# Attention scores contracted over 128 partitions: q's two parts stacked, k's parts doubled, the missing half moved by DMA

## The chip, the cores and the metric

The kernel runs on one core of one Trainium2 chip. The metric is the device time of one execution in microseconds (us); three runs of the kernel before gave 2463.12, 2464.26 and 2464.34 us, so its time is 2464.26 us (median). A profiled execution of it took 2464.76 us.

## The reference

Two transformer blocks run over 512 tokens of width 1024, in float32. The first block mixes with two attentions, a windowed one with grouped heads and a neighbourhood one on a grid of 8 by 64 tokens, and ends in a feed-forward layer. The second has two layers of feed-forward, mixing and feed-forward; each mixing has a causal windowed attention beside a short convolution. Every head has 64 channels (`HEAD_DIM = 64`), every attention has 8 query heads, and the windowed ones have 2 key heads.

```python
def windowed_gqa(q, k, v, sink):            # first block
    ...
        sc = jnp.einsum('bqkgd,bskd->bkgqs', qi, ki).astype(jnp.float32) * scale
...
def neighborhood_attn(q, k, v, rpb):        # first block, 8 key heads
    ...
        sc = jnp.einsum('bchd,brckhd->bhcrk', qr, kn).astype(jnp.float32) * scale
...
def sliding_window_attention(q, k, v, sink):   # second block, each of two layers
    ...
    scores = jnp.einsum("bnqkgd,bnskd->bnkgqs", qb, k_band).astype(jnp.float32) * scale
```

## The kernel before, in words

Activations lie transposed: channels on the 128 partitions, 512 tokens along the free dimension. Every float32 operand of a matmul is split into a high part (rounded to the `fp32r` type by a ScalarE copy) and a low part (what is left, a VectorE subtraction), and a product is the sum of three matmuls: high by high, high by low, low by high. Weights are streamed from HBM in one fixed order (`MIX1_HEAD`, `FILL_AB`, `MIX2_HEAD`, `FILL_C` and others, lines 66 to 78), split the same way (ACT line 376, DVE line 378) some 5 half tiles ahead, and used once.

A linear layer's output tile (`Tile`, lines 450 to 452) is 128 channels by 512 tokens: 8 chunks of the inner dimension, 3 matmuls of 128 rows and 512 columns each. Such a tile of q holds two heads, one on partitions 0 to 63 and one on 64 to 127. `ev_split` (line 859) evacuates it: VectorE multiplies by the norm's factor (`scaled`, lines 846 and 848, or `scaled_by_columns`, line 854), ScalarE rounds the high part (line 553) and VectorE subtracts the low part (line 554). Both parts go into slots, tiles of 128 by 512 named r0 to r51.

Attention is done in steps, each of two heads (index g) and one block of 128 queries: 16 steps each for the windowed attention of the first block ("a"), for the neighbourhood one ("b"), and for each layer of the second block ("c0", "c1"). `qk` (line 704) makes the scores:

```python
for g in range(2):
    r = slice(HD * g, HD * g + HD)
    qs = slice(P * i, P * i + P)
    for j, (a, b) in enumerate(((qh, kh), (qh, kl), (ql, kh))):
        nc.tensor.matmul(sp[:, g, :w], a[r, qs], b[r, sl], start=(j == 0), stop=(j == 2))
```

So a step has six matmuls of 64 rows, three on the upper and three on the lower half of the partitions, with w = 256 columns in a head's first and last block of "a" and "b" and in all of "c", and 384 in the other two blocks of "a" and "b". Then VectorE adds the bias and takes the row's maximum (line 722), ScalarE takes the exponential (line 741), VectorE normalizes (line 749), TensorE transposes (line 758), the two parts are split (lines 553 and 554), and TensorE multiplies by v (line 778).

`run_attention` (line 787) writes the order out. Between the parts of the steps it puts pieces of the linear layers that are due (the "fillers", a quarter of a tile at a time, `halves`), in the order of `FILL_AB` or `FILL_C`, shared evenly over the steps by their cost. Before the first step it puts `2 * head` such quarters. The transposes of a step come one step after its scores in "a" and "b" (`LAG1 = 1`), two steps after in "c" (`LAG2 = 2`). A finished filler is evacuated at the next call of `evacuate`, at the latest just before a step that needs it. Each engine runs its own instructions in the order in which this code issues them.

The head of a mixing stage is `linear2` (line 515): q's first tile, k's tile and v's are made together, with the norm's factor (`inv`) ready only in the middle of v's. GpSimd's queue (POOL) issues the loads of "b"'s bias table (`rpb_load`, line 990), one per block, and later the reloads of x (line 1037).

## Time and profile before

| what | value |
|---|---|
| time, median of 3 runs (lowest to highest) | 2464.26 us (2463.12 to 2464.34) |
| the profiled execution's own time | 2464.76 us |
| its span in the trace | 2463.0 us |
| TensorE busy | 2436.1 us, 99% of the span |
| VectorE busy | 1960.7 us, 80% |
| ScalarE busy | 1261.0 us, 51% |
| GpSimd busy | 24.6 us, 1% |
| granted TensorE clock, mean over the span | 0.996 |

The span is that of the trace; what lies around it makes the execution's own time. Busy shares are of the whole span. Matmuls are pipelined, so one's duration is longer than the step from its start to the next one's, and a busy TensorE is not one at its peak. DVE is VectorE, ACT is ScalarE, PE is TensorE with PEld its weight loads.

### The profile page before, as it was taken

What the parts mean: (1) busy time and instruction counts of PE and PEld (TensorE: products, weight loads), DVE (VectorE), ACT (ScalarE), POOL (GpSimd) and SP (SyncE); (2) the same over time, 40 slices, a digit from 0 to 9 for tenths busy, and PEclk for the clock granted to TensorE, in tenths of its full rate; (3) what the DMA queues carried; (4) which work ended last, traced back from release to release, by engine and by line L of the source; (5) the groups of instructions that cost most, each with busy time, mean ns of one, the idle gap of its engine ahead of it and who ended that gap; (6) DMA issues with size and microseconds to landing.
All of it is one profiled execution on the core that took longest, in us unless ns stands there. A gap on an engine that the chain in (4) does not pass through costs nothing.

```text
span 2463.0 us, 39488 instructions
## 1 busy us (share of the span) xinstructions
PE 2436.1 (99%) x15098; PEld 2167.0 (88%) x15098; DVE 1960.7 (80%) x3943; ACT 1261.0 (51%) x2744; POOL 24.6 (1%) x37
## 2 busy tenths in 40 slices
PE   8999999999999999999999999999999999999998
PEld 6888888999879999988899999899999878999997
DVE  7778678877679878768798888898887687988885
ACT  5554355544455545544565445665445455654454
POOL 2000000000000000000000000000000000000000
PEclk9999999999999999999999999999999999999999
DMA  4222432233322332332223323323333322233332
GB/s 161 69 92 88 118 114 82 94 101 100 106 85 91 101 115 88 114 95 69 84 80 103 107 99 101 102 93 112 98 104 106 102 69 77 75 107 108 106 94 79
DMA packets 73901, 239.45 MB, mean 97 GB/s; under 512 B 8320, under 2 KB 10384, under 8 KB 73712
## 3 DMA queue, kind: packets, MB, share of 16 engines
q1 hardware_dynamic: 70496, 228.10, 29.0%
q0 software_dynamic: 1776, 7.27, 1.0%
q8 instruction: 118, 1.93, 0.3%
q10 hardware_dynamic: 1440, 1.57, 0.2%
q14 instruction: 71, 0.58, 0.1%
HBM read 234.81 MB, written 2.10 MB: 96 GB/s over the span
## 4 chain that ended last, share of the span: by engine, by line
PE 93%; DVE 5%; ACT 1%; issue 0%; DMA 0%; SPq 0%; DVEq 0%; ACTq 0%
PE X L1084 7%; PE X L1083 7%; PE X L1082 7%; PE YZ L1082 5%; PE YZ L1083 5%; PE YZ L1084 5%; PE mlp_D L451 2%; PE mlp_D L450 2%; PE mlp_D L452 2%; PE 0, 'ffn2'_D L450 2%; PE 1, 'ffn1'_D L450 2%; PE 0, 'ffn1'_D L450 2%; PE 0, 'ffn1'_D L451 2%; PE 0, 'ffn2'_D L451 2%; PE 1, 'ffn1'_D L451 2%; PE 0, 'ffn1'_D L452 2%
## 5 line engine op out<-in xcount | busy, mean ns | idle before, releaser
L378 DVE TENSOR_TENSOR wl<-raw,wh 128x512 fp32r<-128x512 f32 (+2 forms) x890 | 531.7, 609 | 98.3 <-ACT wh L376 91.4
L376 ACT CAST wh<-raw 128x512 fp32r<-128x512 f32 (+2 forms) x890 | 469.6, 555 | 8.4 <-DMA raw<-in_w 2.6
L1082 PE MATMUL X<-r,wh 128*128 128x256 f32 x1568 | 445.2, 284 | 3.8 <-ACT g L1088 3.6
L1084 PE MATMUL X<-r,wl 128*128 128x256 f32 x1568 | 444.0, 283 | 0.0
L1083 PE MATMUL X<-r,wh 128*128 128x256 f32 x1568 | 443.9, 283 | 0.0
L376 ACT CAST wh<-s 128x512 fp32r<-128x512 f32 x392 | 242.7, 620 | 224.6 <-DVE s L355 219.2
L1082 PE MATMUL YZ<-r,wh 128*128 128x256 f32 x1176 | 334.4, 284 | 0.8 <-ACT u L1094 0.8
L1083 PE MATMUL YZ<-r,wh 128*128 128x256 f32 x1176 | 333.3, 283 | 0.0
L1084 PE MATMUL YZ<-r,wl 128*128 128x256 f32 x1176 | 333.2, 283 | 0.0
L378 DVE TENSOR_TENSOR wl<-s,wh 128x512 fp32r<-128x512 f32 x392 | 268.8, 686 | 69.5 <-ACT wh L376 67.6
L1082 PEld LDWEIGHTS X<-r,wh 128*128 128x128 f32 x1568 | 300.1, 191 | 15.2 <-ACT g L1088 4.0
L1083 PEld LDWEIGHTS X<-r,wh 128*128 128x128 f32 x1568 | 300.1, 191 | 10.3 <-issue 1.2
L1084 PEld LDWEIGHTS X<-r,wl 128*128 128x128 f32 x1568 | 300.2, 191 | 0.0
L1082 PEld LDWEIGHTS YZ<-r,wh 128*128 128x128 f32 x1176 | 226.3, 192 | 1.6 <-ACT u L1094 1.4
L1083 PEld LDWEIGHTS YZ<-r,wh 128*128 128x128 f32 x1176 | 226.3, 192 | 0.2 <-issue 0.2
L1084 PEld LDWEIGHTS YZ<-r,wl 128*128 128x128 f32 x1176 | 226.3, 192 | 0.0
L1096 ACT COPY g<-X 128x256 f32<-128x256 f32 x98 | 36.5, 372 | 141.6 <-PE X L1084 141.5
L1097 DVE TENSOR_TENSOR u<-u,g 128x256 f32<-128x256 f32 x98 | 41.6, 424 | 75.8 <-ACT g L1096 75.8
L450 PE MATMUL mlp_D<-r,wh 128*128 128x512 f32 x256 | 100.1, 391 | 0.0
L451 PE MATMUL mlp_D<-r,wh 128*128 128x512 f32 x256 | 100.1, 391 | 0.0
L452 PE MATMUL mlp_D<-r,wl 128*128 128x512 f32 x256 | 99.6, 389 | 0.0
L1092 ACT COPY u<-X 128x256 f32<-128x256 f32 x98 | 36.5, 373 | 101.0 <-PE X L1084 101.0
(429 smaller groups left out, 5258.9 us busy)
## 6 DMA issues: line engine op xcount, KB each, us to landing
raw<-in_w SPq DMA_DIRECT2D x320, 512.0 KB, 3.7
raw<-in_w SPq DMA_DIRECT2D x64, 384.0 KB, 3.5
raw<-in_w SPq DMA_DIRECT2D x32, 448.0 KB, 3.5
raw<-in_w SPq DMA_DIRECT2D x32, 320.0 KB, 2.9
raw<-in_w SPq DMA_DIRECT2D x28, 256.0 KB, 2.6
bb<-in_rpb POOLq DMA_DIRECT2D x12, 384.0 KB, 3.3
xt<-in_x POOLq DMA_DIRECT2D x8, 256.0 KB, 2.9
xt<-in_x SPq DMA_DIRECT2D x1, 1024.0 KB, 12.7
```

The source lines that it names most:

```text
L376: nc.scalar.copy(h[:, :w], src)
L378: nc.vector.tensor_tensor(lo[:, :w], src, h[:, :w].bitcast(F32), ALU.subtract)
L450: nc.tensor.matmul(self.ps, h[:, c], hx, start=(self.n == 1), stop=False)
L451: nc.tensor.matmul(self.ps, h[:, c], lx, start=False, stop=False)
L452: nc.tensor.matmul(self.ps, lo[:, c], hx, start=False, stop=end)
L1082: nc.tensor.matmul(out, h[:, c], hx, start=first, stop=False, skip_group_check=skip)
L1083: nc.tensor.matmul(out, h[:, c], lx, start=False, stop=False, skip_group_check=skip)
L1084: nc.tensor.matmul(out, l[:, c], hx, start=False, stop=(k == 3), skip_group_check=skip)
L1092: nc.scalar.copy(u[:, lo], out)
L1096: nc.scalar.copy(g[:, hi], out)
L1097: nc.vector.tensor_tensor(u[:, hi], u[:, hi], g[:, hi], ALU.add)
```

## The change

The product of q and k is written differently. For a head g, one slot now holds q's high part on the head's own 64 partitions and q's low part on the other 64; two slots hold k's high part on both halves and k's low part on both halves. A score is then two matmuls over 128 rows (stacked q by high k, stacked q by low k), which sum all four products of parts instead of three. The halves that the evacuation writes stay where the channels are; the other halves are copied across partitions by DMAs that GpSimd issues (`move`): two per tile of q, four per tile of k, each of 64 partitions by 512 elements (128 KB). A tile of q or k is now rounded and subtracted in two operations of 64 partitions instead of one of 128, and k takes four slots instead of two.

With it come a new order (k ahead of q at the head of a stage and in `FILL_AB`, with the tiles of "b" made earlier) and `head=3` instead of 1: six quarters of fillers instead of two before the first step.

```diff
-MIX1_HEAD = [("qa", 0), ("ka",), ("va",)]
+MIX1_HEAD = [("ka",), ("qa", 0), ("va",)]
 FILL_AB = [("qa", 1), ("qa", 3), ("ga", 0), ("ga", 1), ("qa", 2), ("ga", 2), ("vb", 0), ("ga", 3), ("ga", 4),
-           ("qb", 0), ("kb", 0), ("ga", 5), ("ga", 6), ("qb", 1), ("kb", 1), ("vb", 1), ("ga", 7), ("pa", 0),
-           ("qb", 2), ("kb", 2), ("pa", 2), ("vb", 2), ("pa", 1), ("qb", 3), ("kb", 3), ("vb", 3), ("pa", 4),
+           ("kb", 0), ("qb", 0), ("ga", 5), ("kb", 1), ("qb", 1), ("vb", 1), ("ga", 6), ("kb", 2), ("qb", 2), ("ga", 7),
+           ("vb", 2), ("pa", 0), ("kb", 3), ("qb", 3), ("pa", 2), ("vb", 3), ("pa", 1), ("pa", 4),
            ("pa", 3), ("pa", 6), ("pa", 7), ("gb", 0), ("gb", 1), ("pa", 5)]
-MIX2_HEAD = [("q", 0), ("k",), ("v",)]
+MIX2_HEAD = [("k",), ("q", 0), ("v",)]
...
             for g in range(2):
-                r = slice(HD * g, HD * g + HD)
-                qs = slice(P * i, P * i + P)
-                for j, (a, b) in enumerate(((qh, kh), (qh, kl), (ql, kh))):
-                    nc.tensor.matmul(sp[:, g, :w], a[r, qs], b[r, sl], start=(j == 0), stop=(j == 2))
+                qg, kg = slot[q(c)[g]], k(c)[2 * g:2 * g + 2]
+                for j in range(2):
+                    nc.tensor.matmul(sp[:, g, :w], qg[:, P * i:P * i + P], slot[kg[j]][:, sl], start=(j == 0), stop=(j == 1))
...
-    def run_attention(steps, fillers, needs, head=1, late=False):
+    def run_attention(steps, fillers, needs, head=3, late=False):
...
-    def ev_split(ids, scale=1.0, turn=scaled):
+    def rows(g):
+
+        return slice(HD * g, HD * g + HD)
+
+    def move(out, g_out, src, g_src):
+        nc.gpsimd.dma_start(out.bitcast(F32)[rows(g_out), :], src[rows(g_src), :])
+
+    def ev_q(ids, turn=scaled):
+
         def f(ps):
-            split_act(turn(ps, "evs", scale), slot[ids[0]], slot[ids[1]])
+            t = turn(ps, "evs", QS)
+            for g in range(2):
+                nc.scalar.copy(slot[ids[g]][rows(g), :], t[rows(g), :])
+            for g in range(2):
+                nc.vector.tensor_tensor(t[rows(g), :], t[rows(g), :], slot[ids[g]][rows(g), :].bitcast(F32), ALU.subtract)
+            for g in range(2):
+                move(slot[ids[g]], 1 - g, t, g)
+        return f
+
+    def ev_k(ids, turn=scaled):
+
+        def f(ps):
+            t = turn(ps, "evs")
+            for g in range(2):
+                hi, lo = slot[ids[2 * g]], slot[ids[2 * g + 1]]
+                nc.scalar.copy(hi[rows(g), :], t[rows(g), :])
+                nc.vector.tensor_tensor(lo[rows(g), :], t[rows(g), :], hi[rows(g), :].bitcast(F32), ALU.subtract)
+            for j in range(2):
+                for g in range(2):
+                    i = ids[2 * g + j]
+                    move(slot[i], 1 - g, slot[i].bitcast(F32), g)
         return f
...
-    ka, va = take(2), take(2)
-    linear2(MIX1_HEAD, xop, [ev_split(qa[0], QS), ev_split(ka), ev_v(va)], ar, KC, make_inv)
+    ka, va = take(4), take(2)
+    linear2(MIX1_HEAD, xop, [ev_k(ka), ev_q(qa[0]), ev_v(va)], ar, KC, make_inv)
```

The same is done where "b" and "c" make their q and k.

Three places of the order of instructions follow. The first is TensorE at the first step of attention "a" (sa0 is the tile of its scores; r16 and r17 are q's first slots, r18 and up k's). Before, with the first head's three score matmuls; the second head's read the same:

```order
L452 MATMUL qa_1_373<-r6_94,wl6_254 128x512
L717 MATMUL sa0_392<-r18_106,r16_104 128x256
L717 MATMUL sa0_392<-r19_107,r16_104 128x256
L717 MATMUL sa0_392<-r18_106,r17_105 128x256
L450 MATMUL qa_1_373<-r8_96,wh7_316 128x512
```

Now, with both heads' score matmuls:

```order
L452 MATMUL qa_3_425<-r6_94,wl8_323 128x512
L714 MATMUL sa0_444<-r18_106,r16_104 128x256
L714 MATMUL sa0_444<-r19_107,r16_104 128x256
L714 MATMUL sa0_444<-r20_108,r17_105 128x256
L714 MATMUL sa0_444<-r21_109,r17_105 128x256
L450 MATMUL qa_3_425<-r8_96,wh9_326 128x512
```

Four matmuls stand where six stood, and the step has moved back by four quarters of fillers (24 matmuls of 512 columns) and v's four transposes: it now splits q's tile 3 and not tile 1.

The second is VectorE in step 5 of "a", from the end of its maximum to its normalization (ta5 is the step's tile of probabilities, mxa5 its maxima, evs and evg are evacuated tiles, wl a low part of weights, pta4 the step before's transposes). Before:

```order
L732 TENSOR_TENSOR mxa5_731<-mxa5_731,snk_150 128x2
L846 TENSOR_TENSOR evg_736<-ga_1_598,inv_140 128x512
L378 TENSOR_TENSOR wl20_740<-raw10_378,wh20_739 128x512
L887 TENSOR_TENSOR r29_117<-ya2_679,r28_116 64x256 x2
L554 TENSOR_TENSOR r51_139<-pta4_765,r50_138 128x512
L746 TENSOR_TENSOR dena5_773<-dena5_773,mxa5_731 128x2
L747 RECIPROCAL dena5_773<-dena5_773 128x2
L749 TENSOR_SCALAR ta5_730<-ta5_730,dena5_773 128x384 x2
```

Now:

```order
L729 TENSOR_TENSOR mxa5_775<-mxa5_775,snk_150 128x2
L845 SCALAR_TENSOR_TENSOR evs_780<-qa_2_643,inv_140 128x512
L870 TENSOR_TENSOR evs_780<-evs_780,r28_116 64x512
L870 TENSOR_TENSOR evs_780<-evs_780,r29_117 64x512
L378 TENSOR_TENSOR wl22_789<-raw11_430,wh22_788 128x512
L912 TENSOR_TENSOR r31_119<-ya2_725,r30_118 64x256 x2
L554 TENSOR_TENSOR r51_139<-pta4_808,r50_138 128x512
L743 TENSOR_TENSOR dena5_816<-dena5_816,mxa5_775 128x2
L744 RECIPROCAL dena5_816<-dena5_816 128x2
L746 TENSOR_SCALAR ta5_774<-ta5_774,dena5_816 128x384 x2
```

The evacuation of q's tile 2, with two subtractions of 64 partitions, now stands ahead of this step's softmax where a gate's tile stood.

The third is GpSimd's queue where "b" begins (bb are its bias tables). Before:

```order
L586 TENSOR_TENSOR inv_140<-inv_140,sqa7_234 128x512
L992 DMA bb00_1530<-in_rpb 128x768
L992 DMA bb01_1534<-in_rpb 128x768
L992 DMA bb02_1606<-in_rpb 128x768
```

Now:

```order
L861 DMA r40_128<-r40_128 64x512
L861 DMA r42_130<-r42_130 64x512
L861 DMA r41_129<-r41_129 64x512
L861 DMA r43_131<-r43_131 64x512
L1017 DMA bb00_1554<-in_rpb 128x768
L1017 DMA bb01_1558<-in_rpb 128x768
L861 DMA r28_116<-evs_1565 64x512
L861 DMA r29_117<-evs_1565 64x512
L1017 DMA bb02_1636<-in_rpb 128x768
```

The bias loads, which followed the sums of the first norm directly, now queue behind the moves of k's second tile of "b", and its q's moves behind the first two loads. In all 60 moves have joined the 12 bias loads and 8 reloads on this queue.

## Rows read from the trace of the kernel before

**Rows 1.** The page: busy time, and the chain that ended last, by engine.
```profile
PE 2436.1 (99%) x15098; PEld 2167.0 (88%) x15098; DVE 1960.7 (80%) x3943; ACT 1261.0 (51%) x2744; POOL 24.6 (1%) x37
...
PE 93%; DVE 5%; ACT 1%; issue 0%; DMA 0%; SPq 0%; DVEq 0%; ACTq 0%
```

**Rows 2.** Windows: stages "a" with "b", and "c0"; us, then each engine's busy us.
```profile
30.00:264.00 234.00, 233.47 (x1299) 189.10 (x1298) 180.38 (x490) 116.10 (x298) 6.46 (x12) 1.00 0.26 83
1080.00:1187.00 107.00, 107.00 (x576) 85.49 (x575) 84.88 (x259) 53.02 (x151) 0.00 (x0) 1.00 0.23 71
```

**Rows 3.** The score matmuls, line 717, in "c" and "a": durations in ns, shapes.
```profile
L717 PE MATMUL sc<-r,r x192: 271/277/384, 1086.6 to 2038.1; 64*128 64x256 f32 x192
...
L717 PE MATMUL sa<-r,r x96: 274/332/442, 33.6 to 135.7; 64*128 64x256 f32 x48, 64*128 64x384 f32 x48
```

**Rows 4.** The chain in order of time, 30 to 62 us: start, us, what.
```profile
33.68 0.55 PE sa L717 x6
34.24 0.43 PE qa L450
34.67 0.24 PE qa L451
...
39.07 0.73 PE sa L717 x6
39.80 0.43 PE qa L450
...
48.26 0.71 PE ya L778 x6
...
54.54 1.08 PE ya L778 x9
```

**Rows 5.** Timeline of PE, 33.5 to 33.75 us, two score matmuls.
```profile
33.61 0.39 PE L717 MATMUL sa<-r,r 64*128 64x256 f32 x2
```

**Rows 6.** DVE at q's first evacuation (timeline); 128 against 64 partitions (groups by shape).
```profile
28.25 0.69 DVE L848 SCALAR_TENSOR_TENSOR evs<-qa,inv 128x512 f32<-128x512 f32 x1 [0.21 <-ACT inv L686]
29.63 0.69 DVE L554 TENSOR_TENSOR r<-evs,r 128x512 fp32r<-128x512 f32 x1 [0.69 <-ACT r L553]
...
L1097 DVE TENSOR_TENSOR u<-u,g 128x256 f32<-128x256 f32 x98 | 41.6, 424 | 75.8 <-ACT g L1096 75.8
L887 DVE TENSOR_TENSOR r<-yc,r 64x256 fp32r<-64x256 f32 x32 | 13.5, 421 | 10.7 <-ACT r L886 10.3
```

**Rows 7.** DMA: "b"'s bias loads from POOL (line 992), and 128 KB stores from ACT.
```profile
L992 POOL DMA_DIRECT2D bb<-in_rpb x12: 536/536/562, 82.7 to 222.1; - x12
...
DMA to landing us min/median/max: 3.1/3.3/4.2
...
out<-xt ACTq DMA_DIRECT2D x8, 128.0 KB, 1.8
```

**Rows 8.** Timeline of DVE and PE around step 5 of "a".
```profile
69.56 0.69 DVE L378 TENSOR_TENSOR wl<-raw,wh 128x512 fp32r<-128x512 f32 x1 [1.30 <-ACT wh L376]
...
73.42 0.75 DVE L749 TENSOR_SCALAR ta<-ta,dena 128x384 f32<-128x384 f32 x2
...
75.88 0.82 PE L758 MATMUL pta<-ident,ta 128*128 128x128 f32 x6
```

**Rows 9.** Timeline, DVE and PE at the tightest step of "a", step 13.
```profile
130.97 0.75 DVE L749 TENSOR_SCALAR ta<-ta,dena 128x384 f32<-128x384 f32 x2
...
131.86 0.71 PE L758 MATMUL pta<-ident,ta 128*128 128x128 f32 x5
```

**Rows 10.** Timeline of PE at "b"'s step 12, whose k tile came last.
```profile
229.86 0.38 PE L717 MATMUL sb<-r,r 64*128 64x256 f32 x1 [0.18 <-ACT r L553]
230.59 0.62 PE L717 MATMUL sb<-r,r 64*128 64x256 f32 x5 [0.34 <-DVE r L554]
```

**Rows 11.** Timeline at the first head: the norm's factor, and the first scores.
```profile
27.63 0.59 ACT L686 COPY inv<-spread 128x512 f32<-128x512 f32 x1 [1.29 <-PE spread L674]
...
33.61 0.62 PE L717 MATMUL sa<-r,r 64*128 64x256 f32 x6
```

More of the change, by code (lines that the diff above doesn't have):

```diff
@@ L708, in qk @@
             sp = bank(f"s{kind}{s}", True).rearrange("p (g k) -> p g k", g=2)
-            qh, ql = q(c)
-            kh, kl = k(c)
             w = max(n, 2 * P)
@@ L966, in make @@
                 return halves(key, [pair_of(ya[k]) for k in range(4)], ev_pa(key[1]))
-            ids = take(2)
+            ids = take(4 if key[0] == "kb" else 2)
             {"qa": qa, "qb": qb, "kb": kb, "vb": vb}[key[0]][key[1]] = ids
-            ev = {"qa": lambda: ev_split(ids, QS), "qb": lambda: ev_split(ids, QS, scaled_by_columns),
-                  "kb": lambda: ev_split(ids, 1.0, scaled_by_columns), "vb": lambda: ev_v(ids, scaled_by_columns)}
+            ev = {"qa": lambda: ev_q(ids), "qb": lambda: ev_q(ids, scaled_by_columns),
+                  "kb": lambda: ev_k(ids, scaled_by_columns), "vb": lambda: ev_v(ids, scaled_by_columns)}
             return halves(key, xop, ev[key[0]]())
@@ L1009, in rpb_bias @@
         return bt[:, :, P:] if i == 0 else bt
-    f_a = make_attention("a", ids_pair(qa), lambda c: pair_of(ka), lambda c: pair_of(va),
+    f_a = make_attention("a", qa.get, lambda c: ka, lambda c: pair_of(va),
                          y_plain(ya, lambda c: qa[c] + (ka + va if c == 3 else []), ya_done),
                          alibi("a", 0, 384), 0, (-1, 0, 1))
-    f_b = make_attention("b", ids_pair(qb), ids_pair(kb), ids_pair(vb),
+    f_b = make_attention("b", qb.get, kb.get, ids_pair(vb),
                          y_plain(yb, lambda c: qb[c] + kb[c] + vb[c]), rpb_bias, None, (-1, 0, 1))
@@ L1311, in mix2 @@
         qs, ys, tmp = {0: take(2)}, {}, {}
-        ks, vs = take(2), take(2)
-        linear2([(l,) + k for k in MIX2_HEAD], xop, [ev_split(qs[0], QS), ev_split(ks), ev_v(vs)], ar, 1, make_inv)
+        ks, vs = take(4), take(2)
+        linear2([(l,) + k for k in MIX2_HEAD], xop, [ev_k(ks), ev_q(qs[0]), ev_v(vs)], ar, 1, make_inv)
         cs = [take(2, late=True) for _ in range(4)]
@@ L1342, in make @@
                     qs[key[1]] = take(2)
-                    return halves((l,) + key, xop, ev_split(qs[key[1]], QS))
+                    return halves((l,) + key, xop, ev_q(qs[key[1]]))
                 return halves((l,) + key, xop, ev_conv(*key))
             return (key, 1.0, make)
-        f_c = make_attention(f"c{l}", ids_pair(qs), lambda c: pair_of(ks), lambda c: pair_of(vs),
+        f_c = make_attention(f"c{l}", qs.get, lambda c: ks, lambda c: pair_of(vs),
                              y_plain(ys, lambda c: qs[c] + (ks + vs if c == 3 else [])),
```

## The prediction

> **What bounds the kernel now.** I read the page first: TensorE is busy 99% of the span and holds 93% of the chain that ended last [rows 1]. So the question at each stage is what TensorE saves there, and whether it then has to wait. The windows show the two kinds of stage that the change touches: in 234 us of "a" and "b" TensorE stands idle 0.5 us and VectorE works 180.4 us (77%); in 107 us of "c0" TensorE never stands idle and VectorE works 84.9 us (79%) [rows 2]; "c1" is the same code again. Here a shorter TensorE program is a shorter stage, until VectorE or a transfer makes it wait.
>
> Of the score matmuls [rows 3] the durations say little, since matmuls overlap. The chain in order of time says what they cost [rows 4]. Six score matmuls of 64 rows and 256 columns pass in 0.55 us, and the first weight matmul behind them takes 0.43 us where the next takes 0.24 us: the step's price is 0.55 + 0.43 - 0.24 = 0.74 us. With 384 columns it is 0.73 + 0.43 - 0.24 = 0.92 us. Matmuls of 128 rows and 256 columns (line 778) pass six in 0.71 us and nine in 1.08 us, 0.12 us each. So 64 rows are no cheaper than 128, and entering and leaving them costs extra.
>
> **The scores.** 48 of the 64 steps have 256 columns (16 of "a" and "b" together, 32 of "c"), 16 have 384. Now each has four matmuls of 128 rows. With 256 columns: 4 x 0.12 = 0.48 us, 0.26 us less, times 48 = 12.5 us. For 128 rows and 384 columns the trace has no row. The bounds are the matmul of 256 columns (0.12 us) and that of 512 (0.24 us, line 451 [rows 4]); 384 lies midway, so I take 0.18 us: 4 x 0.18 = 0.72 us, 0.20 us less, times 16 = 3.2 us (7.0 us at 0.12 us, a loss of 0.6 us at 0.24 us). Sum: **15.7 us**, between 11.9 and 19.5 us.
>
> The row that speaks against this is the start of the six: two of them fit in 0.39 us [rows 5], where one alone lasts up to 0.384 us [rows 3], so they began together. Two heads on different halves of the array thus seem to run at the same time. The Trainium skill, in "TensorE: Matmul & The Clock Gate", part 3 on packing small matmuls, says just this: matmuls with a short inner dimension that start on different partitions fall into different row groups and run concurrently, so a lone matmul gains nothing from fewer rows and a pair does. By that rule the change throws a gain away. The trace agrees with the start of the pair and not with the total. Three pairs at the price of one 128-row matmul each would be 0.36 us; the step takes 0.74 us. I go by the 0.74 us.
>
> **The evacuations.** 23 tiles (16 of q, 7 of k) get one more copy on ScalarE and one more subtraction on VectorE, since each is now done in two halves of 64 partitions. A half is no cheaper: 64 partitions by 256 take 421 ns where 128 by 256 take 424 ns [rows 6]. So a subtraction of 512 elements costs 0.69 us as before, and VectorE gets 23 x 0.69 = 15.9 us more: 9.0 us in "a" and "b" (13 tiles), 3.5 us in each "c" (5 tiles). VectorE is idle 53.6 us in the one stage and 22.1 us in the other [rows 2], and ScalarE more. With the stages shortened VectorE's share becomes about 84% (189.4 of 226 us) and 88% (88.4 of 101 us). Over a stage this is covered.
>
> Within a step it need not be. In "a" and "b" a step's transposes come one step behind its scores, and in between VectorE must do what stands in its queue, the evacuation too. What is queued behind the two subtractions is the normalization, and the transposes on TensorE wait for that. In step 5 of "a" the normalization ends at 74.17 us and the transposes begin at 75.88 us, 1.71 us to spare [rows 8]. An evacuation of q there now takes 0.69 us for the scaling, 0.69 us waiting for the copy and 1.38 us for two subtractions [rows 6], 2.8 us in place of a gate's 0.7 us. Of the 2.1 us more, 1.30 us go into a wait that VectorE has there anyway, for a weight copy [rows 8]. That leaves 0.9 us; but this step has lost a quarter of a filler (six matmuls, 1.4 us) and 0.2 us of scores, so TensorE would come some 0.7 us early. The tightest margin is 0.14 us, at step 13 [rows 9], and the evacuation of k that made it tight has moved to step 11, onto a longer stretch of filler. Eleven evacuations fall into steps of "a" and "b". I let three of them cost 0.7 us: **2 us** lost, between none and 2.1 us in each of the eleven, 23 us. In "c" the transposes come two steps behind, and I charge nothing.
>
> One wait goes: "b"'s step 12 had its last q and k tiles just before it, and TensorE stood 0.18 + 0.34 us for their two parts [rows 10]. These tiles are now made earlier. **0.5 us** gained; what would be late next are their moves, below.
>
> **The moves.** 60 DMAs of 128 KB. An issue holds GpSimd 0.54 us [rows 7]; 60 are 32 us on an engine that is busy 24.6 us [rows 1]. What counts is the landing. Bounds: 1.8 us, a 128 KB store from ScalarE's queue, and 4.2 us, the slowest bias load of 384 KB from GpSimd [rows 7]; I take that load's median, 3.3 us, for it is the same queue, issued while VectorE is as busy. The tightest place is the head of a stage. There the norm's factor is ready at 28.2 us [rows 11]. Behind it stand k's scaling, wait and two subtractions and then q's, each 2.6 us by the starts of [rows 6]: 33.4 us; q's two moves issue at 33.4 and 33.9 us and the second lands at 37.2 us (35.7 to 38.1). The scores, at 33.61 us before [rows 11], have moved behind 24 matmuls of 0.23 us: 39.1 us at the earliest. So the cover is 1.9 us, and at the slowest landing still 1.0 us. Without the four quarters each of three heads would wait 3.6 us. The quarters are taken from the steps' share and cost nothing themselves. Elsewhere the distance is longer: for "b"'s last tile of q, 71 matmuls stand between the last of its own and its scores, 36 of 512 columns and 35 of at most 384, some 12.5 us, against about 8 us for evacuation and landing. The bias loads behind k's moves are issued a step after those moves and only VectorE waits for them; I charge nothing, and 3.3 us once if they are late.
>
> **The sum.** 15.7 + 0.5 - 2.0 = 14.2 us less. The profiled execution took 2464.76 us, 1.8 us of it outside the span of 2463.0 us, and lies 0.5 us above the median; the sum is of stages inside the span, so the time becomes 2464.26 - 14.2 = **2450 us**.
>
> **The rivals.**
> 1. VectorE is the new bound of "a" and "b" (slower). Place: the transposes behind the steps with an evacuation. Price: 2.1 us in each of eleven, 23 us, against 16.2 us gained: 2471 us. It decides from 1.5 us per such step on (16.2 / 11). For it speaks the margin of 0.14 us and the share of 84%; against it the 1.30 us of idle time inside a step that looked full. Chance 8%. Half of it, 1 us per step, gives 2459 us, no change: 8%.
> 2. The moves land late. If they took 8.4 us, twice the slowest load, each of three heads would wait 3.2 us beyond its cover, and 9.6 us of the gain would go: 2460 us. Against it: no bias load took over 4.2 us. Chance 5%.
> 3. The two heads do run at once, and the extra time is elsewhere. Then the old step costs 0.36 us (0.54 us with 384 columns), the new one 0.12 us (0.18 us) more: 5.8 + 2.9 = 8.7 us, with the 2 us lost and the 0.5 us gained 2474 us. The rule named above would do this; the 0.74 us of [rows 4] speaks against it. Chance 3%.
> 4. No new wait at all, and 384 columns cost as little as 256: 19.5 + 0.5 = 20 us less, 2444 us. Chance 10%.
>
> My forecast keeps 66%. **Faster** by over 0.2% (4.9 us, about what a measurement of this kernel can tell from no change) are the forecast and rival 4: 76%. Half of rival 1 and rival 2 are the 13% for **no change**, the whole of rival 1 and rival 3 the 11% for **slower**. The range from 2444 to 2460 us takes in rival 4, the bounds on 384 columns, a loss in the steps of up to some 12 us, and late moves.
>
> **What would show it.** Right: six score matmuls and the matmul behind them become four at 0.12 us, with no longer matmul after them; 256 columns give 0.48 us; no wait for a DMA stands at the first scores of a stage; waits of transposes for the normalization sum to about 2 us. Wrong: many such waits in "a" and "b" (rival 1); first scores that begin when a move lands (rival 2); a step of four that is longer than the step of six (rival 3). The forecast also falls if matmuls of 128 rows on these slots don't pass at 0.12 us, as those of line 778 do.

## The result and the profile after

The changed kernel takes **2482.74 us** (median of 4 runs, 2481.93 to 2483.11); the kernel before, beside it on the same chip, 2463.69 us (4 runs, 2463.00 to 2464.34). The ratio is **1.0077, 95% interval 1.0065 to 1.0088**: 19 us slower, where 14 us less were forecast. The profiled execution has a span of 2480.9 us (2463.0 us before), and TensorE's mean granted clock is 0.996 in both; in the attention stages it stays at its upper level (2.4 GHz) throughout in both.

The page of the changed kernel, busy time and the chain that ended last, against [rows 1]:

```profile
PE 2431.2 (98%) x14970; PEld 2176.8 (88%) x14970; DVE 1976.7 (80%) x3966; ACT 1276.7 (51%) x2767; POOL 55.9 (2%) x97
...
PE 78%; DVE 13%; ACT 6%; issue 2%; DMA 0%; SPq 0%; DVEq 0%; ACTq 0%
```

TensorE's share of the chain has fallen from 93% to 78%; VectorE and ScalarE, 6% together before, now hold 19%. The windows of the same two stages, against [rows 2] (us, then busy us of PE, PEld, DVE, ACT, POOL):

```profile
30.00:273.00 243.00, 231.29 (x1233) 195.47 (x1232) 189.65 (x503) 124.29 (x310) 24.86 (x48) 1.00 0.34 99
1089.00:1202.00 113.00, 107.24 (x553) 88.72 (x552) 89.00 (x266) 57.80 (x159) 6.21 (x12) 1.00 0.29 84
```

"a" with "b" now stands 11.7 us idle on TensorE where it stood 0.5, "c0" 5.8 us where it stood none. VectorE's share is what it was: 189.65 of 243 us (78%) and 89.00 of 113 us (79%), against 77% and 79%. The stages have grown with VectorE's work, so its share is about the old one.

**What came as forecast.** The scores, against [rows 4], in the chain in order of time (start, us, what):

```profile
251.97 0.71 PE sb L714 x4
252.68 0.24 PE pa L450
...
258.19 0.47 PE sb L714 x4
258.67 0.23 PE gb L450
258.90 0.23 PE gb L451
```

256 columns cost 0.47 us a step (0.74 before), 384 columns 0.71 us (0.92), and the matmul behind them is no longer than the next. 48 x 0.27 + 16 x 0.21 = 16.3 us are saved on TensorE; 15.7 were forecast. Nor are the moves late. This is POOL's timeline at the first head, the line of all moves with what follows its durations, and PE's timeline at the first scores:

```profile
33.83 0.52 POOL L861 DMA_DIRECT2D r<-evs  x1 [0.20 <-issue]
...
DMA to landing us min/median/max: 2.1/2.4/5.8
...
39.17 0.64 PE L714 MATMUL sa<-r,r 128*128 128x256 f32 x4
```

The last move of the head leaves at 33.83 us (33.9 forecast); the median move lands in 2.4 us, the slowest of all in 5.8 us, beyond the bound of 4.2 us that the forecast took, but not where TensorE waits for it. The scores start at 39.17 us (39.1 forecast) without waiting.

**What did not.** The waits of TensorE, by what it waited for (us in total, times, longest us); of the kernel before this view has 0.5 us for the same lines:

```profile
PE yc L775 <- ACT r L553: 8.0, 8, 1.7
PE pta L755 <- DVE ta L746: 5.4, 7, 1.0
...
PE yc L775 <- DVE r L554: 3.2, 6, 1.0
PE sb L714 <- DVE r L554: 1.9, 2, 1.0
PE vtr L896 <- DVE evv L851: 1.5, 2, 0.8
...
PE ptb L755 <- DVE tb L746: 1.2, 2, 0.7
```

Many short waits, behind VectorE and ScalarE and never a DMA. TensorE's idle time over the whole span has grown by 22.8 us (49.7 against 26.9). That is not all: its busy time has fallen by only 4.9 us, though 16.3 us of scores are saved, so some 11 us more passed while it counts as busy. A matmul of 512 columns lasts 0.39 us and the next one starts 0.23 us after it, so the first 0.16 us of every wait are counted as busy (an estimate from these two numbers); the waits listed are too few to make 11 us of it, and where the rest sits stays open. The dearest group ("yc" waits for the split transposes) is in "c", where nothing was charged. One of them at close range, in the timelines of PE, DVE and ACT in "c0":

```profile
1122.64 0.60 PE L755 MATMUL ptc<-ident,tc 128*128 128x128 f32 x4
...
1129.23 1.11 PE L775 MATMUL yc<-r,r 128*128 128x256 f32 x5 [1.38 <-ACT r L553]
...
1124.94 0.69 DVE L845 SCALAR_TENSOR_TENSOR evs<-0_q,inv 128x512 f32<-128x512 f32 x1
1126.32 1.40 DVE L870 TENSOR_TENSOR evs<-evs,r 64x512 f32<-64x512 f32 x2 [0.69 <-ACT r L868]
1127.75 0.42 DVE L912 TENSOR_TENSOR r<-yc,r 64x256 fp32r<-64x256 f32 x1
...
1125.66 1.26 ACT L868 CAST r<-evs 64x512 fp32r<-64x512 f32 x2 [3.61 <-DVE evs L845]
1126.95 0.37 ACT L911 CAST r<-yc 64x256 fp32r<-64x256 f32 x1
1128.20 0.37 ACT L911 CAST r<-yc 64x256 fp32r<-64x256 f32 x1 [0.88 <-DVE r L912]
1128.59 0.58 ACT L553 CAST r<-ptc 128x512 fp32r<-128x512 f32 x1
```

The four transposes that line 553 copies are through at 1123.24 us (1122.64 + 0.60). ScalarE is idle from 1122.05 us on, but the copy starts at 1128.59 us: in its queue q's evacuation stands ahead, and that waits 3.61 us for VectorE's scaling. Then come two copies of q, a copy of y, the wait for y's subtraction, which stands behind q's two subtractions on VectorE, a second copy of y, and only then the one that TensorE wants. Two engines that are busy half and four fifths of the time hand one piece of work to and fro, and each hand-over is idle time on one of them.

### The profile page after: what moved, and what is told of

It reads as the page before. It is cut to its first block, busy times and chain, and to the rows that moved or that the text cites. A ratio compares the mean times of both kernels' runs of the same rounds, so it can differ in the third digit from the quotient of the medians.

```text
span 2480.9 us, 39456 instructions
## 1 busy us (share of the span) xinstructions
PE 2431.2 (98%) x14970; PEld 2176.8 (88%) x14970; DVE 1976.7 (80%) x3966; ACT 1276.7 (51%) x2767; POOL 55.9 (2%) x97
## 4 chain that ended last, share of the span: by engine, by line
PE 78%; DVE 13%; ACT 6%; issue 2%; DMA 0%; SPq 0%; DVEq 0%; ACTq 0%
PE X L1109 7%; PE X L1108 7%; PE X L1107 7%; PE YZ L1107 5%; PE YZ L1108 5%; PE YZ L1109 5%; DVE wl L378 3%; PE mlp_D L451 2%; PE mlp_D L450 2%; PE mlp_D L452 2%; PE 1, 'ffn1'_D L450 2%; PE 0, 'ffn2'_D L450 2%; PE 0, 'ffn1'_D L450 2%; PE 0, 'ffn2'_D L451 2%; PE 0, 'ffn1'_D L451 2%
```

## The experiments

In the expectations "a filler" or "a step" at the head stands for two quarters of a filler: `head=3` is six quarters, `head=1` two, so the longer head is four quarters more, 24 matmuls or 5.5 us at each of three stages. All ratios are to the kernel before, run on the same chip.

**1. One part alone on the kernel before.**

```diff
-    def run_attention(steps, fillers, needs, head=1, late=False):
+    def run_attention(steps, fillers, needs, head=3, late=False):
```

> The kernel before with one number changed: three steps at the head of each stage without other work instead of one; scores, splits and order stay. H (the later start of the fillers, each then cut into fewer and longer pieces a step, makes the new waits): slower by 9 to 20 us, 2473 to 2484, with new waits of TensorE for y and pta copies. E (the evacuation in halves, 4 instructions more for each q and k tile in the queues of VectorE and ScalarE, makes them): 2462 to 2467, no new waits. S (shorter score steps alone uncover a chain on VectorE and ScalarE that was hidden before): 2462 to 2467 as well.

2473.9 us, ratio 1.0044 (1.0029 to 1.0059): **10.8 us slower**. The head costs by itself, with new waits for y, pta and v's transposes.

```diff
-            split_act(turn(ps, "evs", scale), slot[ids[0]], slot[ids[1]])
+            t = turn(ps, "evs", scale)
+            hi, lo = slot[ids[0]], slot[ids[1]]
+            for g in range(2):
+                nc.scalar.copy(hi[HD * g:HD * g + HD, :], t[HD * g:HD * g + HD, :])
+            for g in range(2):
+                r = slice(HD * g, HD * g + HD)
+                nc.vector.tensor_tensor(lo[r, :], t[r, :], hi[r, :].bitcast(F32), ALU.subtract)
```

> The kernel before with only the evacuation of each q and k tile's high and low parts cut into halves of 64 partitions, two copies on ScalarE and two subtractions on VectorE where there was one each; no moves, scores as before. E: 23 tiles, 0.6 to 0.8 us more in each queue; if most of that stands ahead of a copy that TensorE waits for, slower by 10 to 18 us, 2474 to 2482. H: 2462 to 2467. S: 2462 to 2468, since with longer scores the halves stay covered.

2470.1 us, ratio 1.0027 (1.0017 to 1.0038): **7.0 us slower**, less than the lowest expected. 5.6 us of it lie in "a" and "b", 0.5 us in each "c". So both parts cost while the scores are still long, and neither reaches 19 us.

**2. One part taken out of the changed kernel.** First the head back at 1:

> The changed kernel with one step at the head of a stage, as before. H: the waits of TensorE behind steps (34 us new in all) mostly go, 2448 to 2458, and what may come instead is a wait for the moves at the first scores of a stage, 2 us each at three stages. E and S: 2479 to 2486, waits for y and pta copies as in the changed kernel.

2479.0 us, ratio 1.0063 (1.0048 to 1.0078). Then halves undone, with one copy and one subtraction:

```diff
-            for g in range(2):
-                nc.scalar.copy(slot[ids[g]][rows(g), :], t[rows(g), :])
-            for g in range(2):
-                nc.vector.tensor_tensor(t[rows(g), :], t[rows(g), :], slot[ids[g]][rows(g), :].bitcast(F32), ALU.subtract)
-            for g in range(2):
-                move(slot[ids[g]], 1 - g, t, g)
+            a, b = slot[ids[0]], slot[ids[1]]
+            nc.scalar.copy(a, t)
+            nc.vector.tensor_tensor(t, t, a.bitcast(F32), ALU.subtract)
+            move(b, 1, a.bitcast(F32), 1)
+            move(b, 0, t, 1)
+            move(a, 1, t, 0)
```

> The changed kernel with the split of a q or k tile done over all 128 partitions at once (one copy, one subtraction) and more transfers instead (3 for q, 6 for k, not 2 and 4). E: the waits go for the most part, 2448 to 2460. H and S: 2478 to 2486, waits as in the changed kernel. If the half more transfers come late at a stage's head, 2 us for each of three stages on top, with waits of TensorE at the first scores.

2483.9 us, ratio 1.0084 (1.0069 to 1.0099). Both seem to say that the part taken out cost little. The waits show that something else came in its place; in the first kernel, with a stretch of its windows (us, then busy us of PE, PEld, DVE, ACT, POOL, then the granted clock):

```profile
PE vtr L896 <- DVE evv L851: 5.3, 1, 5.3
PE sc L714 <- DMA r<-evs: 4.9, 3, 2.3
...
PE sa L714 <- DMA r<-evs: 2.3, 1, 2.3
...
168.00:175.00 7.00, 6.33 (x24) 5.76 (x25) 3.27 (x7) 3.10 (x7) 0.18 (x1) 0.54 0.33 112
```

and in the second:

```profile
PE sa L714 <- DMA r<-evs: 4.2, 1, 4.2
...
PE sc L714 <- DMA r<-evs: 3.7, 1, 3.7
...
PE sc L714 <- issue: 3.6, 1, 3.6
```

With a short head the moves are late at all three heads. With whole evacuations there are more moves, and one of each tile overwrites what another still reads and so waits for it.

The last line of the first kernel shows a second thing that came with the waits. TensorE had stood 5.3 us for v's evacuation, and from 168 to 175 us the granted clock is 0.54, near its lower level (1.2 GHz, half of the upper one): a matmul of 512 columns takes 0.43 us there, not 0.23. By windows of 1 us the attention stages ran at the lower level for 13.6 us in all in this kernel and for 17.0 us in the second one, and not at all in the kernel before or the changed one. Half of that at most is time lost, 6.8 and 8.5 us (estimates). So the part was worth more than its removal shows: without the 7.2 us of waits for moves and the clock, the first kernel would stand near 2465 us (an estimate). Experiment 4 prices both parts.

**3. The scores alone, by a third, and what else moves.**

```diff
-                for j, (a, b) in enumerate(((qh, kh), (qh, kl), (ql, kh))):
+                for j, (a, b) in enumerate(((qh, kh), (qh, kl))):
```

> The kernel before with two score products a head, not three, on 64 partitions as before; the product of q's low part with k's high part is left out, so it computes less. Start of the fillers, order, splits and transfers as before. A step has four short multiplications for six, which should shorten it by some 0.25 us, 14 to 18 us over 64 steps. If the steps of the kernel before have room for that (E, H: only halves, head and order eat the gain): 2445 to 2450, next to no new waits. S (shorter steps uncover VectorE and ScalarE by themselves): 2454 to 2463, with TensorE waiting behind steps for pta, y and sb copies.

2456.9 us, ratio 0.9970 (0.9959 to 0.9981): **7.1 us faster**. That lies in the range of theory S, but not for its reason. The chain in order of time shows that the step was shortened less than I had assumed:

```profile
34.18 0.44 PE sa L717 x4
34.61 0.43 PE qa L450
35.04 0.23 PE qa L451
...
44.74 0.55 PE sa L717 x4
45.30 0.43 PE ga L450
45.72 0.23 PE ga L451
```

0.44 + 0.43 - 0.23 = 0.64 us against 0.74 us: 0.10 us, not 0.25. With 384 columns 0.55 + 0.43 - 0.23 = 0.75 against 0.92 us. 48 x 0.10 + 16 x 0.17 = 7.5 us, and 7.1 came out. A small saving is kept almost whole; S in this form falls.

Three more edits of the changed kernel. The old list of fillers in "a" and "b":

```diff
-           ("kb", 0), ("qb", 0), ("ga", 5), ("kb", 1), ("qb", 1), ("vb", 1), ("ga", 6), ("kb", 2), ("qb", 2), ("ga", 7),
+           ("qb", 0), ("kb", 0), ("ga", 5), ("ga", 6), ("qb", 1), ("kb", 1), ("vb", 1), ("ga", 7), ("pa", 0),
...
```

> The changed kernel with the list of fillers in a and b of the kernel before (first q, then k, of each of b's heads; gates and projections between them as before). O (the new list puts evacuations of q and k next to one another and so piles up work on VectorE): stages a and b get 5 to 9 us shorter, 2473 to 2478, c as in the changed kernel. Without O: 2480 to 2486, and at most b's first scores of a head wait for a transfer of k, up to 2 us for each of three heads.

2490.8 us, ratio 1.0111 (1.0095 to 1.0126): worse by 8 us. "b" now waits for moves of k (4.3 us in two waits) and once 5.5 us for v. The new order is no culprit: with the moves in the kernel it saves these waits. The transposes of "a" and "b" one step later:

```diff
-LAG1, LAG2 = 1, 2
+LAG1, LAG2 = 2, 2
```

> The changed kernel with the transposes of a step of a and b two steps behind its scores, as in c, instead of one. If TensorE's 6.6 us of waits for the softmax (pta and ptb) come of too short a distance: these go, 2474 to 2478. If VectorE as a whole has a backlog there (16 us of waits in a and b behind VectorE, whichever instruction shows them): the waits move to y, vtr and score banks, 2479 to 2486. c stays as it is in both.

2491.0 us, ratio 1.0113 (1.0096 to 1.0130). The waits for pta go, and TensorE waits 8.9 us for v's evacuations and 5.9 us for ya instead, longer than expected of either theory. It is not one distance that is too short. (In each of these two kernels the stages ran at the lower clock for 13.6 us, at most 6.8 us of its time.) Last, the two subtractions on GpSimd:

```diff
-                nc.vector.tensor_tensor(t[rows(g), :], t[rows(g), :], slot[ids[g]][rows(g), :].bitcast(F32), ALU.subtract)
+                nc.gpsimd.tensor_tensor(t[rows(g), :], t[rows(g), :], slot[ids[g]][rows(g), :].bitcast(F32), ALU.subtract)
...
-                nc.vector.tensor_tensor(lo[rows(g), :], t[rows(g), :], hi[rows(g), :].bitcast(F32), ALU.subtract)
+                nc.gpsimd.tensor_tensor(lo[rows(g), :], t[rows(g), :], hi[rows(g), :].bitcast(F32), ALU.subtract)
```

> The changed kernel with the subtractions that make the low parts of q and k (two of 64 partitions a tile) on GpSimd instead of VectorE; all else as it is. If VectorE's backlog at evacuations makes the waits: 23 tiles give VectorE back 1.4 us each, the waits in a, b and c fall by half or more, 2462 to 2474, below the kernel before only if nearly all go. If GpSimd slows VectorE beside it or brings the transfers late (its subtraction is likely longer than VectorE's 0.69 us): waits at first scores of a stage, 2478 to 2490.

2483.9 us, ratio 1.0082 (1.0067 to 1.0097): **nothing gained**, though VectorE is busy 27.8 us less. Late moves are little of it: scores wait 1.6 us more than in the changed kernel for moves or without a cause that the profile shows. The place in "c0" shown above, in the timelines of DVE, ACT and PE of this kernel, suggests why:

```profile
1128.52 0.42 DVE L912 TENSOR_TENSOR r<-yc,r 64x256 fp32r<-64x256 f32 x1 [1.72 <-ACT r L911]
...
1126.83 1.26 ACT L868 CAST r<-evs 64x512 fp32r<-64x512 f32 x2 [3.59 <-DVE evs L845]
...
1130.00 0.74 PE L775 MATMUL yc<-r,r 128*128 128x256 f32 x4 [0.97 <-ACT r L553]
```

Where VectorE waited 0.69 us and subtracted for 1.40 us, it now waits 1.72 us: the copy of y stands behind the two copies of q on ScalarE as before.

**4. The parts put on short scores one by one.** The scores get the new shape without stacking, so no halves, moves, longer head or new order are needed:

```diff
-                r = slice(HD * g, HD * g + HD)
...
-                for j, (a, b) in enumerate(((qh, kh), (qh, kl), (ql, kh))):
-                    nc.tensor.matmul(sp[:, g, :w], a[r, qs], b[r, sl], start=(j == 0), stop=(j == 2))
+                for j, (a, b) in enumerate(((qh, kh), (ql, kh)) if g == 0 else ((qh, kl), (ql, kl))):
+                    nc.tensor.matmul(sp[:, g, :w], a[:, qs], b[:, sl], start=(j == 0), stop=(j == 1))
```

> The kernel before with scores of the changed kernel's shape (four multiplications of 128 rows a step), and nothing else: no halves, no transfers, one step at the head, order of before. The stacking is left out: the products mix two heads and the scores are other numbers, so only its time is read. If the gain of the scores is there once nothing else is changed (18 us by TensorE's rows): 2445 to 2449, next to no new waits. If the full gain, twice that of the two products, brings VectorE's chain to light (S): 2450 to 2463 with waits behind VectorE and ScalarE in a, b, c.

2451.0 us, ratio 0.9950 (0.9935 to 0.9965): **12.5 us faster**, three quarters of the 16.3 us. That is just inside the range of theory S, but with few new waits: TensorE's idle time in the trace grows by 2.0 us (28.9 against 26.9). The next three are this kernel with the edits of experiment 1: the head, the halves, both.

> As e9_whole_scores with three steps at the head. If head and scores add up: e9 plus 11 us, as the head cost on the kernel before. If they multiply (VectorE idle at the head, then unable to catch up with shorter steps): e9 plus 18 to 28 us, 2465 to 2476, with most waits in c where the changed kernel has them.

2472.4 us, ratio 1.0037 (1.0024 to 1.0050).

> As e9_whole_scores with the evacuation in halves. If halves and scores add up: e9 plus 7 us. If they multiply: e9 plus 10 to 20 us, in a and b above all. c, with one step at the head, near e9's.

2467.6 us, ratio 1.0017 (1.0007 to 1.0026): the case in which they multiply, but not only in "a" and "b". 9.9 us of the cost lie there, the other 6.4 us later, where "c" was expected to be untouched.

> As e9_whole_scores with both, three steps at the head and halves: the changed kernel but for the transfers and the order of the fillers. If these two and the shorter scores are the whole cause: 2478 to 2487, waits as in the changed kernel. If transfers or the new order cost by themselves: 2460 to 2475.

2487.0 us, ratio 1.0094 (1.0077 to 1.0111). As a table, us against the kernel before:

| | long scores | short scores | cost on long, on short |
|---|---|---|---|
| neither | 0 | -12.5 | |
| longer head | +10.8 | +9.0 | 10.8, 21.5 |
| halves | +7.0 | +4.2 | 7.0, 16.7 |
| both | not run | +23.6 | not run, 36.1 |

On short steps each part costs about twice what it costs on long ones. Together they cost 36.1 us and turn -12.5 into +23.6, and this kernel has no moves at all. The interval of its ratio overlaps that of the changed kernel, whose moves and new order together thus add nothing that these runs can tell.

Some of these costs are the clock's. The stages ran at the lower level for 6.8 us with short scores and the longer head, 3.4 us with the halves and 13.6 us with both; with long scores for 3.4 us with the longer head; in the other kernels of the table not at all. Less half of that, the longer head costs about 9.1 us on long steps and 18.1 on short ones, the halves 7.0 and 15.0, both 29.3 (estimates): the doubling stands.

What the head does is seen in the windows of "c0" with short scores, 25 us each from the end of v on. With two quarters at the head (the first two of its windows; PE, PEld, DVE, ACT busy):

```profile
1078.00:1103.00 25.00, 25.00 (x131) 21.21 (x130) 21.08 (x68) 13.33 (x36) 0.00 (x0) 1.00 0.19 64
1103.00:1128.00 25.00, 25.00 (x138) 21.59 (x136) 20.41 (x66) 12.55 (x38) 0.00 (x0) 1.00 0.27 81
```

and with six (the first three):

```profile
1089.00:1114.00 25.00, 25.00 (x125) 21.05 (x124) 17.18 (x55) 10.64 (x29) 0.00 (x0) 1.00 0.22 69
1114.00:1139.00 25.00, 24.11 (x128) 19.75 (x128) 20.30 (x64) 13.68 (x41) 0.00 (x0) 1.00 0.20 61
1139.00:1164.00 25.00, 23.67 (x128) 20.02 (x127) 20.33 (x66) 12.85 (x40) 0.00 (x0) 1.00 0.24 78
```

The longer head leaves VectorE with 3.9 us less to do in the first 25 us (17.18 against 21.08). It doesn't make that up in this stage: after it both kernels work 20.3 to 20.4 us in 25, the one with TensorE always busy, the other with TensorE waiting. So in these steps VectorE gets no more done, at some 82%, when TensorE waits for it. That 82% is a limit of VectorE is not shown: the first window above has 84%, and in "b" of the kernel with six quarters it works 21.79 of 25 us (200 to 225 us, 87%) with TensorE idle 0.02 us.

**5. Which half of the halves.** On the kernel with short scores, two copies and one subtraction, and then one copy and two subtractions:

```diff
+            for g in range(2):
+                nc.scalar.copy(hi[HD * g:HD * g + HD, :], t[HD * g:HD * g + HD, :])
+            nc.vector.tensor_tensor(lo, t, hi.bitcast(F32), ALU.subtract)
```

> As e9_whole_scores (2451, stacking left out), with the high part of each q and k tile written by two copies of 64 partitions on ScalarE, and one subtraction as before. If the second copy in ScalarE's queue is what the halves cost: 2462 to 2468, near e11's 2468. If it is the second subtraction on VectorE: 2450 to 2455.

2466.4 us, ratio 1.0010 (1.0000 to 1.0019): 15.2 us on top, each against its own kernel before.

> As e9_whole_scores (stacking left out), with one copy and two subtractions of 64 partitions on VectorE. If VectorE's second subtraction is what the halves cost: 2460 to 2468. If ScalarE's second copy: 2450 to 2455. If each costs about half: 2456 to 2461 here and for e13.

2462.5 us, ratio 0.9995 (0.9986 to 1.0005): 11.3 us on top. Each run gave the case in which its own part is the whole cost, yet both together cost 16.7 us, not 26.5. If VectorE simply ran out of time, a second copy on ScalarE would cost nothing. A chain through both engines would explain that the two don't add, and the timeline of the changed kernel shows its lengths: q's first subtraction starts at 1126.32 us, when the first of two copies (1.26 us) is done, and runs beside the second. Copy, copy, subtraction is about 0.6 us longer than copy and subtraction; copy, subtraction, subtraction 0.7 us; and with both halved it is still only 0.7 us, in each of 23 tiles: 14 to 16 us. The intervals, some 2.5 us to either side for these runs and 3.7 us for the kernel with short scores, hardly tell the three costs apart; why the subtraction alone gave the least is not shown.

**6. A smaller version of both parts in the changed kernel.** One copy and one subtraction of 128 partitions for q, plus a copy of the second head's half; three, then four quarters at the head:

```diff
-            for g in range(2):
-                nc.scalar.copy(slot[ids[g]][rows(g), :], t[rows(g), :])
-            for g in range(2):
-                nc.vector.tensor_tensor(t[rows(g), :], t[rows(g), :], slot[ids[g]][rows(g), :].bitcast(F32), ALU.subtract)
+            nc.scalar.copy(slot[ids[0]], t)
+            nc.scalar.copy(slot[ids[1]][rows(1), :], t[rows(1), :])
+            nc.vector.tensor_tensor(t, t, slot[ids[0]].bitcast(F32), ALU.subtract)
```

> The changed kernel with two edits: one copy and one subtraction over all 128 partitions for a q tile plus one copy of the second head's half (transfers as they are, k as it is), and three halves of a filler at the head (one and a half fillers) in place of three fillers. By the sums of the runs so far: 2451 for scores alone, 21 us for two more fillers, so 5 for half a filler, 2 to 5 for what is left of the halves, 0 to 6 for transfers late at three heads: 2456 to 2468. If the head's price does not go in proportion, or transfers are as late as with one filler (4 us at each head): 2468 to 2476.

2478.7 us, ratio 1.0060 (1.0045 to 1.0075): above even the unfavourable case, with moves late at each head (1.4 us in "a", 3.4 us in "c").

> As e15_one_sub_head3h with two fillers at the head. No wait for transfers, and half of the head's 21 us: 2462 to 2470. If the head's price comes mostly with the second filler: 2470 to 2478.

2475.9 us, ratio 1.0049 (1.0034 to 1.0064), the less favourable case. Better by 7 us than the changed kernel, far from 2451: two copies on ScalarE are still there, and they alone cost 15.2 us in experiment 5.

**7. The chain taken off both engines.** The 17 tiles of q and k that are made beside steps are split on GpSimd, copies and subtractions; VectorE keeps the scaling:

```diff
-                nc.scalar.copy(slot[ids[g]][rows(g), :], t[rows(g), :])
+                copy(slot[ids[g]][rows(g), :], t[rows(g), :])
...
-                nc.vector.tensor_tensor(t[rows(g), :], t[rows(g), :], slot[ids[g]][rows(g), :].bitcast(F32), ALU.subtract)
+                vec.tensor_tensor(t[rows(g), :], t[rows(g), :], slot[ids[g]][rows(g), :].bitcast(F32), ALU.subtract)
...
+    pool = (nc.gpsimd.tensor_copy, nc.gpsimd)
...
-            ev = {"qa": lambda: ev_q(ids), "qb": lambda: ev_q(ids, scaled_by_columns),
+            ev = {"qa": lambda: ev_q(ids, scaled, *pool), "qb": lambda: ev_q(ids, scaled_by_columns, *pool),
```

> The changed kernel with the split of the 17 q and k tiles that are made beside steps (both copies and both subtractions) on GpSimd, behind VectorE's scaling; tiles at a stage's head as they are. If the chain of the step through ScalarE's queue makes the waits: 1.2 us of copies go from ahead of the copies that TensorE waits for, the waits of y on ScalarE (8 us) go and those on VectorE fall, 2462 to 2474. If it is VectorE's sum of work or the two fillers at the head alone: no change, as with the subtractions alone, 2480 to 2486. Transfers of b's tiles leave some 4 us later; if that is too late, waits at the first scores of b's heads on top.

2464.0 us, ratio 1.0001 (0.9991 to 1.0010): **18.7 us less than the changed kernel**, as the chain foretold, with the head as long as ever. The waits of TensorE:

```profile
PE yc L775 <- ACT r L553: 2.8, 3, 1.4
...
PE sc L714 <- DMA r<-evs: 2.1, 2, 1.2
...
PE pta L755 <- DVE ta L746: 1.8, 2, 1.0
```

yc behind ScalarE falls from 8.0 to 2.8 us and pta from 5.4 to 1.8. The subtractions alone on GpSimd gave nothing; with the copies it is 20 us. VectorE is as busy as in the changed kernel (1976.2 against 1976.7 us), so it is not the sum of its work that made the waits; ScalarE's queue is 21 us of work shorter.

> As e17_split_on_pool with two fillers at the head. If the chain is short enough now: e17 less 3 to 10 us, 2455 to 2468. If steps are still as long as their chain: e17 less 7 to 11. If TensorE has room again with three fillers already: within 3 us of e17, with waits for transfers at the heads of up to 2 us each.

2462.8 us, ratio 0.9996 (0.9987 to 1.0006): 1.3 us less than with six quarters (3.4 us of the stages at the lower clock with six, 6.8 with four, so up to 1.7 us of the difference is hidden). On short steps with the split on ScalarE and VectorE, four quarters more had cost 21.5 us, or 19.4 with halves; with the split on GpSimd, two of them cost next to nothing. No version that was run and computes the whole attention beats the kernel before.

## Why the prediction was wrong

The sign was wrong, by terms that were put at 2 us and at nothing.

- **Scores, 15.7 us: right.** 16.3 us by the rows after; 384 columns cost 0.71 us (0.72 taken). Of these 12.5 us reach the time when nothing else is changed.
- **Moves, no cost: right, but only behind the longer head, which is dear.** Landing in 2.4 us (3.3 taken), first scores at 39.17 us. Experiment 2 shows what the forecast said of a shorter head: a wait at each of three heads, of 2.3 us at most where it had worked out 3.6.
- **"Over a stage this is covered": the step that failed first.** I took VectorE's idle time (53.6 and 22.1 us) as room and forecast shares of 84% and 88%. They stayed at 78% and 79%, and the stage grew. Waits of VectorE in the windows of "a" with "b", two lines of the kernel before and two of the changed one:

```profile
DVE r L554 <- ACT r L553: 22.2, 38, 2.7
DVE r L887 <- ACT r L886: 9.2, 17, 1.7
...
DVE r L554 <- ACT r L553: 12.9, 21, 2.3
DVE evs L870 <- ACT r L868: 5.5, 8, 0.7
```

Of the 53.6 us, 48.4 were waits for ScalarE (18.3 of the 22.1 in "c0"). The added work did not go into them: VectorE is idle for 53.4 and 24.0 us after the change.
- **"The quarters are taken from the steps' share and cost nothing themselves": wrong.** The longer head costs 10.8 us on the old steps and 21.5 us on the new ones. The quarters were cover for VectorE, which has too little to do at the head and can't catch up.
- **"I let three of them cost 0.7 us", 2 us for the halves: mis-sized.** 7.0 us on the old steps, 16.7 us on the new. The price per step left out ScalarE's second copy, which stands in the queue ahead of the copies that TensorE waits for (15.2 us by itself in experiment 5).
- **"In 'c' the transposes come two steps behind, and I charge nothing": wrong.** The wait in "c" is one step further on: y for the split transposes, behind evacuations in ScalarE's queue, 8.0 us.
- **The 0.5 us at "b"'s step 12** were gained, but at two other steps of "b" the scores now wait 1.9 us behind the subtraction of split transposes (line 554).
- **Rival 1** (8%) had the side and, for "a" and "b", the place: 11.7 us of idle TensorE there, where it priced 23 (waits of 6.6 us stand at the transposes that it named). It missed "c" and the head. I gave it little for one step with 1.30 us to spare; what decides is the sum of the parts that press on one step.
- **Slips in the working that decide nothing.** "c0" less its own 16 x 0.26 us is 102.8 us, not 101, so the share there would have been 86%. k's and q's chains at the head are put at 2.6 us, and the same chain at 2.8 us in the paragraph on the evacuations. 2.1 less 1.30 us leaves 0.8 us, not 0.9.

I had priced three edits apart, each against the old step. The runs show that the prices are not independent: the longer evacuation and the thinner filler cost about twice as much once the step is shorter. Among themselves, on short steps, they about add (36.1 us against 21.5 and 16.7), as if the shorter scores had used up the room that had hidden part of each.

The longer head costs more on short steps (21.5 us) than the 16.6 us of TensorE's work that it moves; up to 3.4 us of that is the clock. Left open: how both parts together would stand on long scores, why VectorE gets no more done in those steps of "c", and where the 11 us sit that count as busy on TensorE.

## What to carry to other kernels

An engine that is idle a fifth of the time has no room if its idle time is waiting for a partner in a loop of hand-overs: look at what share it reaches in the same steps where the bound engine is already waiting, and plan with that, not with 100%. When a change shortens the step of the bound engine, price everything else in it against the new step, and count work moved ahead of the loop as cover taken away. A part that can be taken out without gain may still cost its full price, if what it covered then shows; try it on a kernel that needs no such cover. And look at the granted clock of each run beside its waits: here TensorE ran at half speed behind some of the longer ones, which in some kernels was worth up to 8.5 us (an estimate).

## What the hardware showed that was not expected

**Two heads on different halves of the array do run side by side.** In experiment 3 one matmul less for each head saves 0.10 us with 256 columns: a pair of 64 rows costs what one matmul of 128 rows does (0.12 us), not two. The old step's 0.74 us are three pairs at about 0.12 us and some 0.4 us that two and three pairs have alike. So the rule of the Trainium skill that rival 3 rests on, in "TensorE: Matmul & The Clock Gate", part 3, holds for each pair, and the four matmuls of 128 rows gain all the same, since the fixed part is the larger. Where the fixed part comes from was not tried.

**Beside GpSimd's split some work of VectorE takes more than twice as long.** The normalization of "a" by shape, in the changed kernel:

```profile
L746 DVE TENSOR_SCALAR ta<-ta,dena 128x384 f32<-128x384 f32 x16 | 6.0, 416 | 0.3
...
L743 DVE TENSOR_TENSOR dena<-dena,mxa 128x2 f32<-128x2 f32 x16 | 2.6, 161 | 7.0 <-ACT ta L738 6.5
```

and with the split on GpSimd (experiment 7):

```profile
L746 DVE TENSOR_SCALAR ta<-ta,dena 128x384 f32<-128x384 f32 x16 | 9.1, 608 | 0.3
...
L743 DVE TENSOR_TENSOR dena<-dena,mxa 128x2 f32<-128x2 f32 x16 | 5.4, 339 | 4.4 <-ACT ta L738 3.9
```

The mean goes from 416 to 608 ns, and an addition of two columns from 161 to 339 ns. 34 subtractions of 0.69 us have left VectorE, 23 us, and its busy time is 1976.2 us against 1976.7: the rest has grown by as much. In the timelines of "a" and "b" two normalizations of 384 columns take 0.75 us together in 11 steps, in which GpSimd does nothing then, and 1.65 to 2.71 us in the other 5, all beside one of its copies or subtractions. Which of the two does it is not settled. With the subtractions alone on GpSimd the mean is 420 ns, but in that trace no normalization of 384 columns falls beside one. The Trainium skill, "GPSIMD Engine Reference", section 1, lists GpSimd's memory interface as shared with VectorE, in contention with some of its instructions; the rows with the split on GpSimd agree.
